# Second layer's first modulation product and first expert weights, moved to later tiles of the first output projection

## The chip, the cores and the metric

The kernel runs on one core of a Trainium2 chip. The core has five engines that work side by side: TensorE (PE in the profile, with its weight loads as PEld), VectorE (DVE), ScalarE (ACT), GpSimd (POOL) and SyncE (SP), which here issues nearly all DMAs. Each engine runs its own instructions in the order in which they stand in the program and waits on semaphores for the others. The metric is the time of one execution on the device in microseconds (us).

## The reference

Two layers work on 1024 latent tokens of 1024 channels, with 256 context tokens that the first layer reads. Cut to what matters here:

```
for i in (0, 1):
    sh1, sc1, g1, sh2, sc2, g2 = split(silu(c) @ ada_w[i] + ada_b[i], 6)    # ada_w[i]: 1024 x 6144
    h = modulate(rms_norm(x, norm_mix[i]), sh1, sc1)
    y = even_mixer(h, ...) if i == 0 else short_conv_mixer(h, ...)          # ends in an output projection
    x = x + g1 * y
    h2 = modulate(rms_norm(x, norm_ffn[i]), sh2, sc2)
    x = x + g2 * expert_choice_ffn(h2, router[i], w_gate[i], w_up[i], w_down[i])
return rms_norm(x, norm_final)

def expert_choice_ffn(h, router, w_gate, w_up, w_down):                     # 16 experts, 128 tokens each
    aff = softmax(h @ router)
    gate, idx = top_k(aff.T, 128)
    hid = silu(h[idx] @ w_gate) * (h[idx] @ w_up)
    y = (hid @ w_down) * gate
    return zeros_like(h).at[idx].add(y)
```

The split into six parts is made in three blocks of 2048 columns; block 0 of layer 1 holds `sh1` and `sc1`, which layer 1's first norm needs.

## The kernel before, in words

A product in float32 is made as three products of split operands (high by high, high by low, low by high), at lines 146 to 148. Weights come in granules of 1 MB: a load into a `raw` buffer (line 71, SyncE), a cast to `whi` on ScalarE (line 88), and the rest `wlo` on VectorE or GpSimd (line 89). The `raw` buffers come free when `wlo` has been made, the `whi` and `wlo` buffers when TensorE has used them.

The output projection of layer 0 runs in two passes over the eight tiles of 128 tokens. The second pass is the loop of `start0`: for each tile it loads the partial sum (`ox<-part`, line 664), multiplies (`po`), adds (line 673), transposes the sum (`pt<-ident,ox`, line 276), makes the router's logits (`lg`, lines 282 and 288) and their softmax (`sme`, lines 298 to 322), and writes the tokens' norm to a table (line 323) and the sum to `acc` (line 293). For the last two tiles (`late`) the norm's product is made on ScalarE (line 317) instead of VectorE. Then the tokens of each expert are chosen (lines 335 to 380).

The same loop takes along `ada`, the ten steps of `ada_blocks` for block 0 of layer 1: eight `products`, each of which loads 1 MB of `ada_w` (line 842) and multiplies it into `adsum` on VectorE (lines 845 and 847); `total`, which sums `adsum` over the partitions with four products on TensorE (`pad`, line 855); and `end`, which adds the bias row (line 866) and writes the block to `mods` (line 869). It is read back before layer 1 (`mod_rows<-mods`, line 1900). And it takes along `moe.fetch(early, 4)`, the loads of the first four granules of the first expert (line 71). All these loads take buffers of one pool of four, `raws`.

In `experts`, each expert has 48 products of gate and up (`gu`) on tokens that were gathered (`xg`), transposed on TensorE in two halves (`pt<-ident,xg`, line 411), and split to `xh` (line 140, ScalarE) and `xl` (line 141, VectorE); then the activation `sg`, its transposes (line 486), and 24 products with the down weights (`py`) one expert later. The 24 products of one half need that half's `xh`.

The order of the instructions is not the order of the code. A scheduler takes the instructions that are ready in its own model of time, by priority, where the place in the code is the priority; when a buffer comes free in that model, what waits for it may go ahead of what stands earlier. So a line that stands elsewhere in the code can leave the instructions where they were, and can move others that it has nothing to do with.

Of the kernel before, what the change touches and what calls it, by code (L numbers as in the profile page):

```python
# [648 lines left out]
def split_tile(co, pool, srcs):  # L649
    return split_into(co, *split_tiles(co, pool, sum(src.shape[1] for src in srcs)), srcs)  # L650


def out_project(co, t, mix, ws, x_src, pool, ps, done, half_done=lambda t, x, nh: None, tag="gu", x_pool=None):

    nc = co.nc
    st = {}

    def begin():
        st["mix"] = mix()
        st["x"] = x = (x_pool or pool).tile([P, D], F32, tag="ox", name=co.name("ox"), **({} if x_pool else {"bufs": 3}))
        nc.sync.dma_start(x, x_src[t * P : (t + 1) * P, :])

    def half(nh):
        x, m = st["x"], st["mix"]
        py = ps.tile([P, 512], F32, tag=tag, name=co.name("po"))
        for k, mk in enumerate(m):
            w = ws[nh][k // 4]  # L670
            co.mm3(py, mk, (w[0][:, k % 4, :], w[1][:, k % 4, :]), k == 0, k == len(m) - 1)
        sl = slice(nh * 512, (nh + 1) * 512)
        nc.vector.tensor_tensor(x[:, sl], x[:, sl], py, op=ALU.add)
        half_done(t, x, nh)

    return [begin, lambda: half(0), lambda: half(1), lambda: done(t, st["x"])]
# [896 lines left out]
def hybrid_dit_kernel(stack, tc, aps):  # L1573
# [29 lines left out]
    with ExitStack() as sa:  # L1603
# [71 lines left out]
        ada = [ada_steps(*b, sums, raws, ps, "ad", 4) for b in ((0, 1), (0, 2))] + [[]]  # L1675
# [152 lines left out]
    def start0(make, wpb, pool, ps, _):  # L1828
        moe = make()
        early = Weights(co, raws, wpa)  # L1830
        ada = ada_steps(1, 0, pool, raws, ps, "tr")
        x_pool = Cycle((Bufs(out_pool, 3), 3), (Bufs(pool, 2), 2))
        for i, (t, srcs) in enumerate(pass2.items()):
            for step in ada[2 * i : 2 * i + 2]:
                step()
            if i == 4:
                moe.fetch(early, 4)
            for step in out_project(
                co, t, lambda: split_tile(co, out_pool, srcs), ws, part, out_pool, ps,
                lambda t, x, late=i > 5: moe.route_tile(t, x, pool, ps, late), lambda t, x, nh: moe.route_half(t, x, nh, pool, ps), x_pool=x_pool,  # L1840
            ):
                step()
        mix0.close()
        kept_raws.insert(0, (stack.enter_context(pooled("more", 2, "right")), 2))
        return moe
# [69 lines left out]
    def mixed_raws():  # L1915
# [3 lines left out]
        return kept_cycle[0]  # L1919

    xs, moe0 = feed_forward(0, lambda wpb: None, start0, before_last)
    kept_splits.append(stack.enter_context(pooled("wps", 1, "right")))

# [70 lines left out]
```

## Time and profile before

| | us |
|---|---|
| median of 3 runs | 1860.47 |
| lowest and highest | 1858.13 and 1872.29 |
| the profiled execution's own time | 1875.52 |
| its span, first to last instruction | 1873.8 |

The page of the profile gives TensorE busy 1658.2 us (88% of the span), its weight loads 1338.6 us (71%), VectorE 1275.1 us (68%), ScalarE 903.3 us (48%), GpSimd 530.5 us (28%). The chain of work that ended last lies on TensorE for 47% of the span and on VectorE for 10%. Busy shares are means over stages that differ; a stage is read from its own window and from what ends the waits in it. The profiled execution took 15.05 us more than the median of the runs.

### The profile page before, as it was taken

To read this page: it belongs to the slowest core of one execution; us is meant where nothing else is said; L and a number is where in the kernel's file an instruction comes from. 1 tells how busy PE (TensorE), PEld (TensorE's weight loads), DVE (VectorE), ACT (ScalarE), POOL (GpSimd) and SP (SyncE) were. 2 spreads that over 40 slices of the span, in tenths; PEclk is the share of its full clock that TensorE was granted. 3 is DMA by queue.
4 is the path that set the end of the run, shared out by engine and by line. 5 is a ranking of instruction groups with operands and counts; after the bars stand their busy time and mean duration, and the time that the engine had idled before them with its cause. 6 is when DMAs were issued, how large, how long until landed. Compare 5 with 4: busy or idle time off the path is not lost.

```text
span 1873.8 us, 26253 instructions
## 1 busy us (share of the span) xinstructions
PE 1658.2 (88%) x9617; PEld 1338.6 (71%) x9617; DVE 1275.1 (68%) x1966; ACT 903.3 (48%) x1581; POOL 530.5 (28%) x549
## 2 busy tenths in 40 slices
PE   6999997878888893999989989999999769998995
PEld 2988875667886772778767767788887547776784
DVE  4628786656679766779778867354253558987897
ACT  3645332522753245878666552011132457876663
POOL 4310287462324027122111352000012432321123
PEclk7999999869998995899999999999999869998998
DMA  7517664648494957899999666531264369999995
GB/s 280 155 47 227 209 203 130 170 136 269 128 347 150 382 196 256 295 321 399 383 319 343 182 214 243 189 116 45 88 236 139 140 243 328 381 399 330 333 317 202
DMA packets 187671, 443.73 MB, mean 237 GB/s; under 512 B 46521, under 2 KB 108714, under 8 KB 158870
## 3 DMA queue, kind: packets, MB, share of 16 engines
q1 hardware_dynamic: 178470, 408.76, 61.0%
q0 software_dynamic: 9072, 33.30, 7.2%
q8 instruction: 76, 1.25, 0.3%
q14 instruction: 53, 0.43, 0.1%
HBM read 368.65 MB, written 73.35 MB: 236 GB/s over the span
## 4 chain that ended last, share of the span: by engine, by line
PE 47%; DVE 10%; issue 8%; DMA 7%; ACT 4%; POOL 1%; SPq 1%; DVEq 0%; ACTq 0%; POOLq 0%
PE pin L146 4%; PE pin L147 4%; PE pin L148 4%; PE gu L148 4%; PE gu L147 4%; PE gu L146 4%; PE po L146 3%; PE po L148 3%; PE po L147 3%; PE py L146 2%; PE py L147 2%; PE py L148 2%; DVE wlo L89 2%; ACT whi L88 2%; ACT oh L394 2%
## 5 line engine op out<-in xcount | busy, mean ns | idle before, releaser
L89 DVE TENSOR_TENSOR wlo<-raw,whi 128x2048 fp32r<-128x2048 f32 (+3 forms) x248 | 481.0, 1962 | 118.7 <-ACT whi L88 118.4
L88 ACT CAST whi<-raw 128x2048 fp32r<-128x2048 f32 (+3 forms) x268 | 423.7, 1613 | 210.4 <-PE pin L147 77.7
L146 PE MATMUL gu<-whi,xh 128*128 128x512 f32 x512 | 208.1, 409 | 17.7 <-ACT xh L140 16.9
L147 PE MATMUL gu<-wlo,xh 128*128 128x512 f32 x512 | 207.7, 406 | 3.1 <-DVE wlo L89 3.1
L148 PE MATMUL gu<-whi,xl 128*128 128x512 f32 x512 | 202.6, 409 | 0.2 <-DVE xl L141 0.2
L147 PE MATMUL pin<-h1T,whi 128*128 128x512 f32 x384 | 150.4, 393 | 0.0
L148 PE MATMUL pin<-h1T,wlo 128*128 128x512 f32 x384 | 150.2, 393 | 0.0
L146 PE MATMUL pin<-h1T,whi 128*128 128x512 f32 x384 | 148.9, 396 | 0.0
L522 POOL DMA_INDIRECT acc<-y,idx x31 | 80.0, 2579 | 209.9 <-DVE y L516 194.5
L400 POOL DMA_INDIRECT xg<-table,idx x32 | 57.8, 1806 | 286.3 <-ACT idx L398 272.6
L146 PEld LDWEIGHTS gu<-whi,xh 128*128 128x128 f32 x512 | 99.7, 195 | 39.5 <-ACT xh L140 19.2
L147 PEld LDWEIGHTS gu<-wlo,xh 128*128 128x128 f32 x512 | 99.4, 194 | 25.9 <-DVE wlo L89 5.0
L148 PEld LDWEIGHTS gu<-whi,xl 128*128 128x128 f32 x512 | 98.9, 193 | 20.5 <-DVE xl L141 0.6
L847 DVE SCALAR_TENSOR_TENSOR adsum<-raw,cs,adsum 128x512 f32<-128x512 f32 (+1 forms) x77 | 95.5, 1241 | 25.9 <-DMA raw<-in_ada_w_dram 25.5
L89 POOL TENSOR_TENSOR wlo<-raw,whi 128x1024 fp32r<-128x1024 f32 (+2 forms) x20 | 67.4, 3416 | 155.0 <-ACT whi L88 154.8
L146 PE MATMUL py<-whi,hh 128*128 128x512 f32 x256 | 102.5, 407 | 2.5 <-DVE y L516 1.3
L147 PE MATMUL py<-wlo,hh 128*128 128x512 f32 x256 | 102.0, 399 | 0.0
L148 PE MATMUL py<-whi,hl 128*128 128x512 f32 x256 | 101.7, 399 | 0.0
L146 PE MATMUL pq<-hT,whi 128*128 128x512 f32 (+1 forms) x256 | 97.0, 379 | 1.7 <-ACT last L1150 1.1
L148 PE MATMUL pq<-hT,wlo 128*128 128x512 f32 (+1 forms) x256 | 96.6, 377 | 0.0
L147 PE MATMUL pq<-hT,whi 128*128 128x512 f32 (+1 forms) x256 | 96.1, 376 | 0.0
L146 PE MATMUL po<-whi,mh 128*128 128x512 f32 x224 | 92.9, 416 | 3.0 <-ACT mh L140 2.3
(402 smaller groups left out, 3729.3 us busy)
## 6 DMA issues: line engine op xcount, KB each, us to landing
raw<-in_w_gate_dram SPq DMA_DIRECT2D x64, 1024.0 KB
raw<-in_w_up_dram SPq DMA_DIRECT2D x64, 1024.0 KB
raw<-in_w_down_dram SPq DMA_DIRECT2D x64, 1024.0 KB
raw<-in_ada_w_dram SPq DMA_DIRECT2D x32, 1024.0 KB
raw<-in_ada_w_dram SPq DMA_DIRECT2D x64, 256.0 KB
raw<-in_sc_w_in_dram SPq DMA_DIRECT2D x12, 1024.0 KB
table<-h SPq DMA_DIRECT2D x16, 520.0 KB
raw<-in_ev_w_in_dram SPq DMA_DIRECT2D x16, 512.0 KB
```

Source lines behind the costliest of these rows:

```text
L88: nc.scalar.copy(hi[:, part], raw[:, part])
L89: (lo_engine or e).tensor_sub(lo[:, part], raw[:, part], hi[:, part])
L146: nc.tensor.matmul(out, lhs[0], rhs[0], start=start, stop=False)
L147: nc.tensor.matmul(out, lhs[0], rhs[1], start=False, stop=False)
L148: nc.tensor.matmul(out, lhs[1], rhs[0], start=False, stop=stop)
L394: nc.scalar.activation(oh[:, t, :], co.places, AF.Sign, bias=before)
L400: nc.gpsimd.indirect_dma_start(out=xg, out_offset=None, in_=self.table[:, :], in_offset=bass.IndirectOffsetOnAxis(ap=idx, axis=0))
L522: self.scattered = self.nc.gpsimd.indirect_dma_start(out=self.acc[:, :], out_offset=bass.IndirectOffsetOnAxis(ap=idx, axis=0), in_=y, in_o ...
L847: nc.vector.scalar_tensor_tensor(st["sum"], raw, cs[:, k, 0:1], st["sum"], op0=ALU.mult, op1=ALU.add)
```

## The change

The ten steps of `ada` are taken two per tile: before in the first five turns of the loop (tiles 3, 4, 2, 5, 1), now in the last five (tiles 5, 1, 6, 0, 7). The call that fetches four granules moves from the fifth turn to the seventh.

```diff
         for i, (t, srcs) in enumerate(pass2.items()):
-            for step in ada[2 * i : 2 * i + 2]:
+
+            for step in ada[2 * (i - 3) : 2 * (i - 2)] if i >= 3 else []:
                 step()
-            if i == 4:
+            if i == 6:
                 moe.fetch(early, 4)
             for step in out_project(
```

Three places show what became of it in the order of the instructions.

First, SyncE in the second pass, where the last loads of `ada_w` and the first granules stand. Before:

```order
L842 DMA raw_7185<-in_ada_w_dram 128x2048
L842 DMA raw_7188<-in_ada_w_dram 128x2048
L71 DMA raw_7285<-in_w_gate_dram 128x2048
L664 DMA ox_7013<-part 128x1024
L1780 DMA part<-ox_6790 128x1024
L71 DMA raw_7287<-in_w_up_dram 128x2048
L293 DMA acc_79<-ox_6920 128x1024
L71 DMA raw_7289<-in_w_gate_dram 128x2048
L71 DMA raw_7291<-in_w_up_dram 128x2048
```

Now:

```order
L842 DMA raw_7446<-in_ada_w_dram 128x2048
L842 DMA raw_7449<-in_ada_w_dram 128x2048
L71 DMA raw_7452<-in_w_gate_dram 128x2048
L664 DMA ox_6997<-part 128x1024
L1780 DMA part<-ox_6790 128x1024
L71 DMA raw_7454<-in_w_up_dram 128x2048
L293 DMA acc_79<-ox_6910 128x1024
L71 DMA raw_7456<-in_w_gate_dram 128x2048
L71 DMA raw_7458<-in_w_up_dram 128x2048
```

The names have other numbers, and the rows are the same: each load stands where it stood, and so it is with all eight loads of `ada_w`. On SyncE the one row of the pass that moved is `mods<-adrows`, from ahead of the third of the eight `table` rows to behind the fourth. On VectorE the eight products stand where they stood, and the row of line 866 stands 25 rows later; on TensorE the four `pad` products stand some 55 rows later, still inside the pass, and the transposes and logits of the last tiles are laid out a little differently.

Second, TensorE in layer 0's experts, at the first tokens of expert 10 (`pt_9412` and `xh_9417` are its first half, `sg_9466` is the activation of expert 9, `py` is expert 8's down product). Before:

```order
L411 MATMUL pt_9412<-ident,xg_9031 128x128 x4
L146 MATMUL gu_9544<-whi_9548,xh_9417 128x512
L147 MATMUL gu_9544<-wlo_9549,xh_9417 128x512
L146 MATMUL gu_9545<-whi_9566,xh_9417 128x512
L147 MATMUL gu_9545<-wlo_9567,xh_9417 128x512
L411 MATMUL pt_9457<-ident,xg_9031 128x128 x4
L146 MATMUL py_9482<-whi_9472,hh_9346 128x512
L147 MATMUL py_9482<-wlo_9473,hh_9346 128x512
L148 MATMUL py_9482<-whi_9472,hl_9347 128x512
```

Now:

```order
L411 MATMUL pt_9412<-ident,xg_9031 128x128 x4
L146 MATMUL gu_9544<-whi_9548,xh_9417 128x512
L147 MATMUL gu_9544<-wlo_9549,xh_9417 128x512
L146 MATMUL gu_9545<-whi_9566,xh_9417 128x512
L147 MATMUL gu_9545<-wlo_9567,xh_9417 128x512
L411 MATMUL pt_9457<-ident,xg_9031 128x128 x4
L486 MATMUL pt_9511<-ident,sg_9466 128x128 x4
L148 MATMUL gu_9544<-whi_9548,xl_9418 128x512
L146 MATMUL gu_9544<-whi_9548,xh_9417 128x512
L147 MATMUL gu_9544<-wlo_9549,xh_9417 128x512
```

Up to the second row of transposes nothing moved since the pass. Then the activation of expert 9 is transposed ahead of expert 8's down products, and 17 products of expert 10 follow it. From here the two programs differ. Between the transposes of an expert's first half and the first product that uses them stood, for experts 9 to 13, 0, 0, 1, 20 and 11 products; now 0, 0, 24, 21 and 21.

Third, TensorE in layer 1's experts, where expert 8's first half is transposed (`pt_14774`, which becomes `xh_14779`; `xh_14654` is expert 7). Before:

```order
L148 MATMUL gu_14736<-whi_14785,xl_14655 128x512
L146 MATMUL gu_14736<-whi_14785,xh_14654 128x512
L411 MATMUL pt_14774<-ident,xg_14393 128x128 x4
L147 MATMUL gu_14736<-wlo_14786,xh_14654 128x512
L148 MATMUL gu_14736<-whi_14785,xl_14655 128x512
L146 MATMUL gu_14737<-whi_14803,xh_14654 128x512
L147 MATMUL gu_14737<-wlo_14804,xh_14654 128x512
```

Now:

```order
L411 MATMUL pt_14774<-ident,xg_14393 128x128 x4
L148 MATMUL gu_14737<-whi_14803,xl_14655 128x512
L146 MATMUL gu_14737<-whi_14803,xh_14654 128x512
L147 MATMUL gu_14737<-wlo_14804,xh_14654 128x512
L148 MATMUL gu_14737<-whi_14803,xl_14655 128x512
L411 MATMUL pt_14819<-ident,xg_14393 128x128 x4
L146 MATMUL gu_14906<-whi_14910,xh_14779 128x512
L147 MATMUL gu_14906<-wlo_14911,xh_14779 128x512
L146 MATMUL gu_14907<-whi_14928,xh_14779 128x512
L147 MATMUL gu_14907<-wlo_14929,xh_14779 128x512
```

Before, 14 products stood between those transposes and the first one that uses `xh_14779`; now 4 do. For experts 8 to 13 of layer 1 the numbers were 14, 0, 0, 1, 20 and 11; now they are 4, 4, 15, 0, 21 and 0.

## Rows read from the trace of the kernel before

**Rows 1.** Stages: us, busy (x) of PE, PEld, DVE, ACT, POOL; PEclk, DMA, GB/s.

```profile
636.00:712.00 76.00, 68.49 (x434) 50.10 (x433) 53.94 (x113) 31.16 (x86) 21.73 (x15) 0.97 0.64 248
...
753.00:1062.00 309.00, 293.46 (x1386) 238.58 (x1387) 258.20 (x183) 226.22 (x269) 63.12 (x29) 0.96 0.92 335
...
1524.00:1843.00 319.00, 303.26 (x1441) 246.34 (x1442) 265.43 (x190) 229.09 (x280) 67.70 (x30) 0.97 0.91 326
```

**Rows 2.** Waits of SyncE in layer 0's experts: us in total, times, longest.

```profile
SPq L71 <- DVE wlo L89: 218.1, 69, 11.2
```

**Rows 3.** Waits of ScalarE in the same stretch.

```profile
ACT whi L88 <- PE py L148: 28.6, 14, 6.8
...
ACT whi L88 <- PE gu L148: 10.9, 7, 2.9
```

**Rows 4.** TensorE in layer 0's experts: [idle before <-releaser].

```profile
965.21 0.50 PE L146 MATMUL gu<-whi,xh 128*128 128x512 f32 x1 [0.44 <-ACT xh L140]
...
967.08 0.74 PE L411 MATMUL pt<-ident,xg 128*128 128x128 f32 x4 [0.67 <-ACT idx L398]
968.52 0.71 PE L486 MATMUL pt<-ident,sg 128*128 128x128 f32 x4 [0.69 <-DVE xl L141]
...
1005.31 0.50 PE L146 MATMUL gu<-whi,xh 128*128 128x512 f32 x1 [1.28 <-ACT xh L140]
...
1007.91 0.55 PE L147 MATMUL gu<-wlo,xh 128*128 128x512 f32 x1 [1.63 <-DVE wlo L89]
```

**Rows 5.** TensorE in layer 1's experts, the same.

```profile
1687.83 0.79 PE L146 MATMUL gu<-whi,xh 128*128 128x512 f32 x1 [2.64 <-ACT xh L140]
...
1690.20 0.80 PE L147 MATMUL gu<-wlo,xh 128*128 128x512 f32 x1 [0.72 <-DVE wlo L89]
...
1710.41 0.75 PE L411 MATMUL pt<-ident,xg 128*128 128x128 f32 x4 [0.87 <-DVE hl L141]
1714.06 0.51 PE L146 MATMUL gu<-whi,xh 128*128 128x512 f32 x1 [2.91 <-ACT xh L140]
...
1716.97 0.80 PE L146 MATMUL py<-whi,hh 128*128 128x512 f32 x1 [0.55 <-DVE y L516]
...
1776.84 0.49 PE L146 MATMUL gu<-whi,xh 128*128 128x512 f32 x1 [0.82 <-ACT whi L88]
```

**Rows 6.** SyncE's queue in order of time: start us, us, DMA issue.

```profile
578.44 0.33 SPq L842 DMA_DIRECT2D raw<-in_ada_w_dram  x1
...
636.78 3.33 SPq L842 DMA_DIRECT2D raw<-in_ada_w_dram  x2
642.06 0.33 SPq L71 DMA_DIRECT2D raw<-in_w_gate_dram  x1
...
686.41 0.55 SPq L869 DMA_DIRECT2D mods<-adrows  x1
...
697.09 0.32 SPq L323 DMA_DIRECT2D table<-h  x1
...
734.79 0.38 SPq L1900 DMA_DIRECT2D mod_rows<-mods  x1
```

**Rows 7.** VectorE in order of time, the last ada product and its sum.

```profile
653.13 2.35 DVE L847 SCALAR_TENSOR_TENSOR adsum<-raw,cs,adsum 128x2048 f32<-128x2048 f32 x1
...
685.70 0.68 DVE L866 TENSOR_TENSOR adrows<-adrows,pad 128x512 f32<-128x512 f32 x1
```

**Rows 8.** TensorE in order of time, the pass of layer 0.

```profile
684.49 1.04 PE L855 MATMUL pad<-adsum,ones 128*32 128x512 f32 x8
```

**Rows 9.** ScalarE in order of time, the last tiles of that pass.

```profile
709.82 1.13 ACT L317 ACTIVATE h<-ox,rstd 128x1024 f32<-128x1024 f32 x1
710.86 0.39 ACT L307 ACTIVATE sme<-sme,sm 128x128 f32<-128x128 f32 x1
```

**Rows 10.** Two windows in layer 1's experts, columns as in rows 1.

```profile
1710.00:1720.00 10.00, 6.14 (x19) 4.57 (x20) 7.95 (x8) 4.75 (x6) 4.26 (x2) 0.74 0.96 351
1720.00:1730.00 10.00, 10.00 (x50) 8.20 (x50) 4.51 (x3) 6.45 (x12) 0.00 (x0) 0.92 0.74 207
```

## The prediction

> **What bounds the kernel now.** I read the stages first. In the second pass TensorE is busy 68.49 of 76.00 us, and VectorE 53.94 [rows 1]: the pass is TensorE's, and work that is put elsewhere inside it finds no hole to fill. The eight loads and products that the edit names are the smaller matter there; the experts that follow are the larger, since they take 309 us in layer 0 and 319 us in layer 1 with TensorE busy 293.46 and 303.26 [rows 1]. What is left to win or lose in them is 15.5 and 15.7 us of idleness, and the half clock that comes with it.
>
> Then I asked who waits for whom there. SyncE's loads of weights wait for `wlo`, 69 times and 218.1 us [rows 2], so the transfers are held back by buffers that are full. ScalarE's casts wait for TensorE's products, 28.6 and 10.9 us [rows 3], and no row has them wait for a load. So TensorE sets the pace, and the splits and the loads follow it. Last I read what TensorE itself waits for: the `xh` of tokens that it transposed just before [rows 4, 5].
>
> **The loads and the products of the modulation: 0.** The code asks for them three tiles later, but the order shows all eight loads and the four early granules in the rows where they stood, and the eight VectorE products too. The first load is issued at 578.44, before the second pass begins, and the last pair from 636.78 on, with the first granule at 642.06 [rows 6]. What lets them go is a free buffer, and that is the same as before. The last product starts at 653.13 and takes 2.35 us [rows 7], and stays. I put nothing on it. Bounds: nothing excludes that a load meets a wait of another kind, but no row on SyncE ahead of it differs, so both ends are 0.
>
> **The sum over partitions and its write: 0, between -1.0 and +1.0.** The four `pad` products take 1.04 us [rows 8], and stand some 55 rows later now. A step of 1.04 us that moves within a stretch in which TensorE is the bound changes nothing; at most it falls into an idle gap (-1.04) or delays the last tile by itself (+1.04). The row of line 866, at 685.70 [rows 7], moves 25 rows down; it takes 0.68 us of a VectorE that is busy 71% here (53.94 of 76.00 us [rows 1]). The write to `mods` was issued at 686.41; it now follows the fourth `table` row, which was issued at 697.09, and the block is read back at 734.79 [rows 6]. So it is still some 37 us early. Queued behind it on SyncE are `table` and `acc` rows of the last tiles, whose data come later than the sum of line 866.
>
> **The last tiles: 0, between -1.0 and +1.1.** Before, the two late tiles end together: the second tile's exponent waits at 709.82 until the first tile's norm product of 1.13 us is through, and starts at 710.86 [rows 9]. Now one late tile is done whole on ScalarE ahead of the other's softmax. If it comes 1.04 us earlier, the wait goes (-1.04); if not, the other's softmax waits for the product's 1.13 us. The rows speak for neither, so I take 0.
>
> **Layer 0's experts: -3.1, between -4.7 and +2.9.** Up to expert 10's first transposes TensorE's rows are the same. From there on the transposes of experts 11, 12 and 13 have 24, 21 and 21 products behind them before their tokens are wanted, where 1, 20 and 11 stood. A window of 10 us at nearly full clock holds 50 products, some of them small [rows 10], so one takes 0.2 us at least and 21 take 4.2 us, more than the longest such wait, 2.91 [rows 5]. The waits in this stretch are 0.44, 0.67 and 0.69 around 965 us, which hang on expert 11's transposes, 1.28 at 1005.31 on expert 13's, and 1.63 at 1007.91 on a `wlo` [rows 4]. The first four go: 0.44 + 0.67 + 0.69 + 1.28 = 3.08. The fifth is a split and need not; with it 4.71. On the other side, expert 9's activation is now transposed right behind another transpose and 17 products of expert 10 come ahead of the down products that covered them; if their `xl` or a split is late, that is one wait of the usual size, 2.9.
>
> **Layer 1's experts: +1.6, between -6.7 and +14.5.** Here the same spots cost, before, for expert 9: 2.64 + 0.72 = 3.36; for expert 10: 0.87 + 2.91 + 0.55 = 4.33; for expert 11 the three waits of layer 0 repeat, 0.44 + 0.67 + 0.69 = 1.80 [rows 4]; for expert 13: 0.82 [rows 5]. In all 10.3 us. Now experts 11 and 13 have nothing between the transposes and their first use, and experts 8 and 9 have four products; experts 10 and 12 have 15 and 21 and should be free. A spot with nothing between cost 3.36 to 4.33 where ScalarE had casts of weights ahead of the `xh`, as it has in the new order, so 3.85 each; four products of 0.2 us take 0.8 off a wait of 2.9, which leaves 2.1 each. 2 x 3.85 + 2 x 2.1 = 11.9, and 11.9 - 10.3 = +1.6. Low end: all four spots as cheap as half of expert 11's, 0.9 each: 3.6 - 10.3 = -6.7. High end: each spot at the full price of expert 10's, where the window from 1710 holds 19 products against 50 in the next one, at a granted clock of 0.74 (the engine ran at 1.2 GHz for part of it, right after it had stood idle) [rows 10]: (50 - 19) / 50 x 10 = 6.2 us, and 4 x 6.2 - 10.3 = +14.5.
>
> **The sum.** 0 + 0 + 0 - 3.1 + 1.6 = -1.5 us. Against the profiled execution's own 1875.52 that is 1874.0. That execution lies 15.05 above the median and above the slowest of the three runs, so I carry the difference and not the time: 1860.47 - 1.5 = 1859.0. A measurement of this kernel can tell about 1%, or 18.6 us, from no change (its own three runs lie 14.2 apart), and the sum is a tenth of that.
>
> **The rivals.** *Layer 1 pays (slower).* The mechanism is the half clock behind a short wait: each of the four spots in experts 8 to 13 costs 6.2 us as expert 10 did. For it: the window from 1710 [rows 10]. Against it: only one spot of four went so before, and expert 11's cost 1.80. It decides from the third spot at full price on: two at 6.2 and two at 2.1 are 16.6, or +6.3. At the full +14.5 with -3.1 in layer 0 it gives 1872. The Trainium skill, "TensorE: Matmul & The Clock Gate", section "HAM oscillation — how this bites in real kernels", says that a wait that recurs throttles the array each time, so that every turn starts at the slow clock. By that rule every one of the four spots is dear, and 1872 would be the forecast; the trace agrees at expert 10 and does not at expert 11, which cost 1.80.
>
> *The short waits all go (faster).* Layer 0 gains 4.7, the pass 1.0, and layer 1's spots are cheap, 6.7: 1860.5 - 12.4 = 1848. For it: TensorE is the bound, so each wait counts whole. Against it: ScalarE's order in layer 1 puts up to five casts ahead of expert 11's `xh`.
>
> *The transfers set the pace of the experts, and nothing moves.* Then a wait that goes on TensorE comes back as a wait for weights: 1860.5. For it: the DMA share is 0.92 and 0.91 [rows 1]. Against it: 335 and 326 GB/s, and loads that wait for buffers [rows 1, 2]. The Trainium skill, "Perfetto Trace Analysis", section "Roofline", puts the ceiling of one core at its 16 DMA engines, about 435 GB/s in all. By that figure the stage has a quarter of the rate left, and this rival falls; the trace agrees so far as no cast waits for a load.
>
> *The change does what it says on the chip after all*, and the loads come three tiles later: excluded by the order, which the queues follow.
>
> **How the numbers follow.** My forecast, 1859, with its neighbours from 1852 to 1866: 0.55. Layer 1 pays, 1866 to 1877: 0.17. The waits all go, 1846 to 1852: 0.12. Transfers set the pace, 1860.5: 0.10. What I have not seen, on either side, the loads that move among it: 0.06. The lows add up to -1.0 - 1.0 - 4.7 - 6.7 = -13.4, or 1847; the highs, +1.0 + 1.1 + 2.9 + 14.5 = +19.5, or 1880, which needs all of them at once. The range is 1846 to 1876. Faster by over 1% would be under 1842, more than all the lows: 0.07. Slower by over 1% is above 1879, only at the end of the highs: 0.07. Within 1%: 0.86.
>
> **What would show it.** In the profile after: the `ada_w` loads from about 578 to 640 and the last `adsum` at about 653, as before; the `pad` product near 700; the choice of tokens starting within 1.5 us of 712; in layer 0's experts no waits for `xh` behind expert 10; in layer 1's, waits at experts 8, 9, 11 and 13 and none at 10. I am wrong if the loads move, if the pass ends more than 2 us elsewhere, or if the two stages of experts change by more than 5 and 15 us; then the coupling of ScalarE's casts with TensorE's releases does more than these rows show.

## The result: slower by 0.57%, 10.6 us

Of 20 runs each, the changed kernel takes 1876.6 us in the median (1869.24 to 1881.56) and the kernel before 1863.7 (1858.13 to 1872.29). The ratio is 1.0057, with a 95% interval from 1.0045 to 1.0068: 10.6 us, from 8.4 to 12.7 (the two medians by themselves lie 12.9 us apart). I had forecast 1859, a gain of 1.5 us, with a range up to 1876. I had started from 1860.47, the median of three runs of before; with 20 it is 1863.7, so 3.2 us of the distance to 1876.6 lie in the start and not in the change. I had also put the least that can be told at about 1%; the interval reaches some 0.1% to each side. The profiled execution of after took 1879.88 us, its span is 1878.0.

The stages of after, in windows as in [rows 1], each moved to where the stage now begins:

```profile
632.00:708.00 76.00, 69.08 (x434) 50.73 (x433) 54.00 (x113) 31.46 (x88) 22.89 (x15) 0.97 0.67 251
748.00:1057.00 309.00, 292.07 (x1397) 235.64 (x1398) 259.14 (x187) 225.89 (x269) 68.69 (x29) 0.97 0.92 335
1518.00:1837.00 319.00, 297.63 (x1403) 239.73 (x1404) 259.54 (x184) 228.99 (x279) 63.33 (x29) 0.96 0.90 324
```

In these windows the pass and layer 0's experts look much as they did; the second window ends before the last products of layer 0, of which more below. In layer 1's experts TensorE gets through 1403 instructions in 319 us, where it got through 1441 [rows 1]. The loss is there.

SyncE's queue of after, in order of time:

```profile
574.56 0.33 SPq L842 DMA_DIRECT2D raw<-in_ada_w_dram  x1
...
632.66 3.33 SPq L842 DMA_DIRECT2D raw<-in_ada_w_dram  x2
637.93 0.33 SPq L71 DMA_DIRECT2D raw<-in_w_gate_dram  x1
...
698.52 0.55 SPq L869 DMA_DIRECT2D mods<-adrows  x1
```

VectorE of after, the last product of the modulation and the row of line 866:

```profile
649.09 2.35 DVE L847 SCALAR_TENSOR_TENSOR adsum<-raw,cs,adsum 128x2048 f32<-128x2048 f32 x1
...
697.80 0.69 DVE L866 TENSOR_TENSOR adrows<-adrows,pad 128x512 f32<-128x512 f32 x1 [0.44 <-PE pad L855]
```

The loads, the granules and the products stand as before, 4 us earlier on this execution's clock [rows 6, 7]; only the sum and the write to `mods` are later, by 12 us on the clock and so by 16 against the rest. The choice of tokens, its first row (line 335) and the row `dg` (line 352) on VectorE, before:

```profile
712.14 1.28 DVE L335 TENSOR_SCALAR_CACHE_REDUCE junk<-v,cand 128x1024 bf16<-128x1024 f32 x1
...
732.08 2.30 DVE L352 TENSOR_SCALAR dg<-ident,cand 128x16 f32<-128x16 f32 x1
```

And in after:

```profile
708.14 1.28 DVE L335 TENSOR_SCALAR_CACHE_REDUCE junk<-v,cand 128x1024 bf16<-128x1024 f32 x1
...
728.07 0.85 DVE L352 TENSOR_SCALAR dg<-ident,cand 128x16 f32<-128x16 f32 x1
```

From the first load to the first row of the choice of tokens it is 133.58 us (708.14 - 574.56) and was 133.70 (712.14 - 578.44). So what the change names costs nothing. From that row to layer 0's first product, though, the six executions with after's order there (after, force11to13, undo_l1, undo_swap, undo_early, copies_late_after) take 39.5 to 39.7 us, and the eleven with before's 41.1 to 42.5: some 2.2 us are won. The row `dg` is where it shows: it takes 0.74 to 0.90 us in the six and 2.30 to 3.66 in the eleven, and ends 0.03 us behind a split of weights on GpSimd (`wlo`, line 89) in all seventeen. In the six that split begins 3.6 to 3.8 us ahead of `dg`, in the eleven 0.9 to 2.2.

To compare experts across executions I count the products with gate, up and down weights (lines 146 to 148, 1152 in each layer) in the timeline. Layer 1, in us, with the experiments that follow; the two columns of us are from one profiled execution of each kernel:

| kernel | ratio to before, 95% interval | 1st to 577th product | 577th to last |
|---|---|---|---|
| before | 1 | 154.6 | 164.5 |
| after | 1.0057 (1.0045 to 1.0068) | 159.7 | 170.0 |
| fetch5 | 0.9999 (0.9981 to 1.0017) | 155.4 | 164.0 |
| fetch6 | 0.9995 (0.9976 to 1.0013) | 152.2 | 163.9 |
| force11to13 | 1.0084 (1.0059 to 1.0110) | 158.7 | 171.6 |
| force_late | 1.0065 (1.0042 to 1.0087) | 158.6 | 168.6 |
| undo_l1 | 0.9999 (0.9982 to 1.0016) | 153.1 | 164.1 |
| do_l1 | 1.0058 (1.0040 to 1.0076) | 159.1 | 171.7 |
| do_early | 1.0036 (1.0017 to 1.0055) | 158.4 | 164.1 |
| do_late | 1.0028 (1.0014 to 1.0041) | 151.2 | 170.0 |
| do_swap | 1.0025 (1.0007 to 1.0042) | 155.1 | 164.2 |
| undo_swap | 1.0052 (1.0034 to 1.0070) | 153.8 | 170.1 |
| do_rest | 1.0018 (0.9998 to 1.0039) | 158.5 | 162.7 |
| undo_early | 1.0030 (1.0010 to 1.0050) | 151.6 | 169.1 |
| copies_late | 0.9947 (0.9928 to 0.9966) | 149.9 | 165.2 |
| copies_late_after | 1.0005 (0.9985 to 1.0026) | 148.7 | 168.7 |
| copies_turn | 1.0047 (1.0032 to 1.0063) | 148.6 | 171.8 |

TensorE in layer 1's experts in after, the waits at the first products of expert 1 (experts count from 0) and at experts 9, 10, 11 and 13:

```profile
1534.97 0.51 PE L146 MATMUL gu<-whi,xh 128*128 128x512 f32 x1 [1.48 <-ACT xh L140]
...
1537.41 0.80 PE L148 MATMUL gu<-whi,xl 128*128 128x512 f32 x1 [1.24 <-DVE xl L141]
...
1686.98 0.67 PE L147 MATMUL gu<-wlo,xh 128*128 128x512 f32 x1 [2.30 <-DVE wlo L89]
...
1708.19 0.50 PE L146 MATMUL gu<-whi,xh 128*128 128x512 f32 x1 [1.45 <-ACT xh L140]
...
1731.70 0.79 PE L146 MATMUL gu<-whi,xh 128*128 128x512 f32 x1 [2.84 <-ACT xh L140]
...
1735.31 1.13 PE L411 MATMUL pt<-ident,xg 128*128 128x128 f32 x4 [1.53 <-DVE xl L141]
...
1776.62 0.51 PE L146 MATMUL gu<-whi,xh 128*128 128x512 f32 x1 [2.00 <-ACT xh L140]
...
1779.06 1.04 PE L411 MATMUL pt<-ident,xg 128*128 128x128 f32 x4 [1.24 <-DVE xl L141]
```

Counted off, the row at 1686.98 is the 604th product, in expert 9; the one at 1708.19 is the 673rd, the first of expert 10; those at 1731.70 and 1776.62 are the 745th and the 889th, the first of experts 11 and 13. So of the spots that I had named, 9, 11 and 13 wait. Expert 8, for which I had put 2.1 us, waits for nothing, and expert 10, which I had put down as free, waits 1.45 us for `xh`. The 15 products of the order do stand between its transposes and their use. But on ScalarE the cast to `xh`, at 1707.58, comes behind three casts of weights and these rows:

```profile
1705.23 2.45 ACT L394 ACTIVATE oh<-places,aff 128x128 f16<-128x128 f16 x8
```

The first two rows of the list I had not foreseen: before's profile shows none for `xh` or `xl` at that place. ScalarE there, before:

```profile
1531.41 1.91 ACT L88 CAST whi<-raw 128x2048 fp32r<-128x2048 f32 x1 [0.99 <-issue]
1533.71 1.92 ACT L88 CAST whi<-raw 128x2048 fp32r<-128x2048 f32 x1 [0.39 <-PE gu L148]
1538.34 0.19 ACT L403 COPY aff<-xg 128x1 f32<-128x1 f32 x1 [2.71 <-DMA xg<-table,idx]
1538.44 0.58 ACT L140 CAST xh<-pt 128x512 fp32r<-128x512 f32 x1
```

And in after:

```profile
1524.73 1.92 ACT L88 CAST whi<-raw 128x2048 fp32r<-128x2048 f32 x1 [0.61 <-issue]
1532.44 0.19 ACT L403 COPY aff<-xg 128x1 f32<-128x1 f32 x1 [5.79 <-DMA xg<-table,idx]
1532.54 1.90 ACT L88 CAST whi<-raw 128x2048 fp32r<-128x2048 f32 x1
1534.34 0.58 ACT L140 CAST xh<-pt 128x512 fp32r<-128x512 f32 x1
```

Two neighbours have changed places. The copy of a gathered gate (line 403) waits for its gather; before, the second cast of weights was done in that time. Now the cast stands behind the copy: ScalarE stands still for 5.79 us, and `xh` comes 1.90 us after the copy instead of right after it.

The same has happened once more, some 80 us after the first product: the copy of expert 6's gate has gone ahead of a cast of weights that stood ahead of it. The copy before, and then in after:

```profile
1604.76 0.19 ACT L403 COPY aff<-xg 128x1 f32<-128x1 f32 x1 [5.06 <-DMA xg<-table,idx]
```

```profile
1601.64 0.19 ACT L403 COPY aff<-xg 128x1 f32<-128x1 f32 x1 [6.77 <-DMA xg<-table,idx]
```

### The profile page after: what moved, and what is told of

The parts are those of the page before. It is cut to its first block, busy times and chain, and to the rows that moved or that the text cites. A ratio compares the mean times of both kernels' runs of the same rounds, so it can differ in the third digit from the quotient of the medians.

```text
span 1878.0 us, 26243 instructions
## 1 busy us (share of the span) xinstructions
PE 1656.6 (88%) x9617; PEld 1334.0 (71%) x9617; DVE 1277.8 (68%) x1966; ACT 903.3 (48%) x1581; POOL 534.1 (28%) x549
## 5 line engine op out<-in xcount | busy, mean ns | idle before, releaser
L89 POOL TENSOR_TENSOR wlo<-raw,whi 128x1024 fp32r<-128x1024 f32 (+2 forms) x20 | 66.8, 3387 | 151.7 <-ACT whi L88 151.6
```

The costliest lines, as they stand in the source:

```text
L89: (lo_engine or e).tensor_sub(lo[:, part], raw[:, part], hi[:, part])
```

## The experiments

### The granules' half, and transposes put earlier

The first theory (A) was the prediction's own rival: the late spots of layer 1 cost more than I had put on them. **fetch5** and **fetch6** are the kernel before with the fetch alone moved:

```diff
-            if i == 4:
+            if i == 6:
                 moe.fetch(early, 4)
```

(`i == 5` in fetch5.)

> The kernel before with the fetch of four granules one tile later (at i == 5), the products left alone. The order of the instructions is the same as before's on all five engines. Both theories: ratio 1.000, between 0.9985 and 1.0015. It shows what the measurement tells from nothing, and its trace is a second sample of before's order: if the first eight experts of layer 1 take 153.6 us to their 576th product as before, the 159.7 us of after are the change's; if they take up to 160, they are scatter of single executions.

> Only the second half of the change: the fetch at i == 6, the eight products where they were. The order keeps the pad products and the mods write ahead as before, and gives layer 1's experts the order of after, instruction for instruction; layer 0's from expert 10 on nearly so. Theory A (the order of the late experts costs it): as after, ratio 1.004 to 1.007. Theory B (it is the moved modulation in the pass, or the first experts of layer 1 as they follow from it): ratio 1.000 to 1.002, since pad and mods stand as before.

Both came out as before, 0.9999 and 0.9995. The expectation of fetch6 is wrong on the order: with the fetch alone moved, the rows of all five engines are before's, as with fetch5. So its time says nothing between A and B. It shows that the moved fetch by itself does nothing, and gives a third sample of before's order. The three take 152.2 to 155.4 us to the 577th product of layer 1, and after 159.7. Single executions of one order do scatter there: undo_swap and do_rest below have the same rows up to expert 7 and take 153.8 and 158.5.

**force11to13** is after, and **force_late** before, with transposes held ahead of the products of the expert before (in force_late the condition is experts 8 to 15 of both layers; the lines that hand over the two instructions are left out):

```diff
-                        co.mm3(pa, (hi[:, k, :], lo[:, k, :]), (g[0][:, k, :], g[1][:, k, :]), half == k == 0, half == 1 and k == 3)
+                        mm = co.mm3(pa, (hi[:, k, :], lo[:, k, :]), (g[0][:, k, :], g[1][:, k, :]), half == k == 0, half == 1 and k == 3)
+                        if self.li and e in (10, 11, 12) and half and rows and k == 0:
+                            co.order(self.turn, mm)
```

> The kernel after, with one constraint on TensorE's order in layer 1 only: the transposes of the first half of experts 11, 12 and 13 stand ahead of the second-half products of the expert before, so that 24 products lie between them and their first use instead of 0, 21 and 0. Theory A: the two spots of 4.2 and 3.6 us by the trace go, 5 to 8 us of the 10.6, ratio 1.001 to 1.003. Theory B: the spots are as cheap as the prediction's sum had them beside before's own, and the ratio stays at 1.005 to 1.006.

> The kernel before, with that constraint for experts 8 to 15 of both layers: 24 products at least between the first half's transposes and their use, where before has 14, 0, 0, 1, 20 and 11. Theory A: the waits for xh of both layers go with the half clock behind them, 4.7 us in layer 0 and 10.3 in layer 1 by the waits alone: ratio 0.990 to 0.994, faster than both kernels. Rival (transfers and splits set the pace, and TensorE's waits only come back in another place): 0.998 to 1.002.

Theory A foresaw gains, and neither has one: force11to13 is at 1.0084 where after is at 1.0057, and force_late at 1.0065 where before is at 1. In force_late the waits for `xh` in the late experts went, and others came. TensorE in force_late, in layer 1 from expert 7 on:

```profile
1676.04 1.13 PE L412 MATMUL pt<-ident,xg 128*128 128x128 f32 x4 [4.27 <-DVE hl L141]
...
1750.70 0.51 PE L147 MATMUL gu<-wlo,xh 128*128 128x512 f32 x1 [1.97 <-DVE wlo L89]
...
1853.19 0.79 PE L563 MATMUL plast<-xl,xh 128*128 128x512 f32 x1 [4.65 <-DVE raw L565]
```

The early transposes wait 4.27 us for `hl`: they write a buffer of the pool `tr`, which has two, and `hl` still reads one. Then the splits are late (`wlo`), and the sums after the last expert. But each constraint also made the scheduler lay out other rows anew, so neither run says what a spot costs. That called for kernels in which nothing else moves.

### Layer 1 in a given order

The next eight kernels hold every engine in an order that is written down, from layer 1's choice of tokens on: before's, after's, or a mixture. The edges bind the issue order only.

```diff
+def pin_orders(tc, nc):
...
+    for rows in json.loads(zlib.decompress(base64.b85decode(PINNED))).values():
+        for earlier, later in zip(rows, rows[1:]):
+            tc.add_manual_dep(traced[base + later], traced[base + earlier].name, no_wait, reason="order")
...
         hybrid_dit_kernel(tc, args)
+        pin_orders(tc, nc)
```

> The kernel after, with the instructions of layer 1 (from its choice of tokens on) held on every engine in the order of the kernel before; the pass, layer 0 and the mixer stay as in after. Theory C (all of the loss is layer 1's order, its first experts included): ratio 0.999, between 0.997 and 1.001. Rival P (the pass with the moved pad and mods, or layer 0, causes it): as after, 1.0045 to 1.0068.

> The converse: the kernel before, with layer 1 held in the order of after; everything ahead of it as before. Theory C: ratio 1.006, between 1.004 and 1.008. Rival P: 0.9985 to 1.0015.

**undo_l1** gives 0.9999 and **do_l1** 1.0058. Theory C holds and rival P falls: the whole loss is the order of layer 1, and what stands in front of it comes out even.

**do_early** and **do_late** divide it between experts 4 and 7, where both orders agree.

> The kernel before, and of after's order in layer 1 only what lies in the first three experts: two swaps of neighbours on VectorE, three on ScalarE, three moves on TensorE. The first of them puts the copy of a gathered row's gate, which waits for the gather, ahead of a cast of weights on ScalarE. By the traces after is 5 us behind at the 480th product (135.1 against 130.0, 130.8 and 127.7 us). Theory C1 (a copy that waits for a transfer, with casts behind it, costs several us): ratio 1.0025, between 1.0015 and 1.004, with waits for xh and xl of some 2.7 us near 17 us after the first product. Theory C2 (only the late experts count): 0.999 to 1.001, and the 5 us are scatter.

> The kernel before, and of after's order in layer 1 only what lies from expert 7 on. By the traces the stretch from the 576th to the last product takes 170.0 us in after and 164.5, 164.1 and 163.9 in three executions of before's order. Theory C1: ratio 1.003, between 1.0015 and 1.0045, so that the two parts add up to do_l1. Theory C2: 1.0045 to 1.007, all of it. My recorded sum put it at +1.6 us, which would be 1.001.

1.0036 and 1.0028: both parts count, together 1.0064 beside do_l1's 1.0058. TensorE of do_early, at the place of after's first two waits:

```profile
1528.04 0.50 PE L146 MATMUL gu<-whi,xh 128*128 128x512 f32 x1 [1.16 <-ACT xh L140]
...
1530.48 0.80 PE L148 MATMUL gu<-whi,xl 128*128 128x512 f32 x1 [1.24 <-DVE xl L141]
```

C1 named these two waits with 2.7 us near 17 us after the first product; they are 2.40 us, at 16.3 and 18.8. In the traces the parts do not overlap. To the 577th product the six executions with before's first experts take 151.2 to 155.4 us (mean 153.0), the four with all of after's 158.4 to 159.7 (159.0; force11to13 is one). From the 577th on, seven with before's late experts take 162.7 to 164.5 (163.9), five with after's 169.1 to 171.7 (170.2).

### One pair of neighbours

**do_swap** is before with the pair on ScalarE exchanged, **undo_swap** is after with it put back, **do_rest** is do_early without it, and **undo_early** is after with all early moves put back. The edit of do_swap, in the rows of ScalarE's order:

```diff
 L88 CAST whi_13765<-raw_13763 128x2048
-L88 CAST whi_13783<-raw_13781 128x2048
 L403 COPY aff_13619<-xg_13621 128x1
+L88 CAST whi_13783<-raw_13781 128x2048
 L140 CAST xh_13655<-pt_13650 128x512
```

> The kernel before, with one pair of neighbours exchanged and nothing else: on ScalarE, in layer 1's first expert, the copy of a gathered gate (line 403, it waits for a gather) now stands ahead of one cast of weights (line 88), as in after. TensorE keeps before's order, so that the two products that after has put ten places later meet the late cast at once. Theory C1 (a waiting copy with a cast behind it): ratio 1.003, between 1.0015 and 1.005, most of do_early's 1.0036. Theory C3 (the copy gives up only time that ScalarE has, and the other small moves make the loss): 0.9985 to 1.001.

> The kernel after, with that one pair put back and all else of layer 1 held as in after. Theory C1: the 5.6 us that the first experts lose go for the most part, ratio 1.0028, between 1.001 and 1.0045. Theory C3: as after, 1.005 to 1.007.

> do_early without the exchanged pair: the kernel before with the other small moves of after's first three experts in layer 1. Theory C1 (the pair carries the early loss): 0.9995 to 1.0015. Theory C4 (the other moves carry half of it or more): 1.002 to 1.004.

> The kernel after with all moves of layer 1's first three experts put back, the late experts in after's order. Both theories: 1.0028 as do_late, between 1.0015 and 1.004, if the parts add up; beside undo_swap's 1.0052 it shows what the other moves cost in after. If it comes out near 1.005 too, the early part costs after nothing and the parts do not add up.

do_swap costs 0.0025, as C1 had it. do_rest costs 0.0018 with an interval down to zero, between the two theories. undo_early is at 1.0030, where both had it. undo_swap is at 1.0052, against C1, though in its trace the two waits are gone and the 577th product comes at 153.8 us. That execution is the fastest of its six, and the ratio stays unexplained. By the ratios alone it is open how the early loss divides.

The traces divide it. From the 1st to the 73rd product of layer 1, the five executions with the pair exchanged (after, do_l1, do_early, do_swap, force11to13) take 24.7 to 26.7 us (mean 25.5), and the nine without it, the copies in their old places, 20.5 to 21.9 (21.2). The pair costs 4.3 us, or 0.0023. And do_rest, which was to show the other moves without a copy, is not without one: it keeps the second copy ahead of its cast, where ScalarE waits 7.51 us in its trace. From the 289th to the 361st product the six executions with that second pair exchanged (after, do_l1, do_early, undo_swap, do_rest, force11to13) take 20.1 to 22.2 us (20.8), and the eight without 18.3 to 20.1 (19.0): 1.8 us. The two make 6.1 us, as much as the 6.0 that the first experts lose. Between the two stretches these groups of six and eight scatter by 3 us and differ by 0.2 in the mean; behind them, force_late apart, they agree within 0.1. So do_rest does not tell C1 from C4.

### The copies out of the way

In **copies_late** and **copies_late_after** the order of before, or of after, is held from layer 0's choice of tokens on, and each gate copy is put behind the second `xh` cast of its own expert:

```diff
+    rows = pinned["Activation"]
+    for copy, casts in tc.gates:
+        if at[copy.name] in rows:
+            rows.remove(at[copy.name])
+            rows.insert(rows.index(at[casts[1].name]) + 1, at[copy.name])
```

> The kernel before, its order held, with all 32 gate copies of both layers moved down on ScalarE, each behind the second xh cast of its own expert, which needs the same gather. Theory C1: the 35 us in which ScalarE stands before gathers go, and with them the waits of TensorE that hang on casts in the first experts of each layer, some 2 to 4 us in each: ratio 0.9965, between 0.994 and 0.999, faster than both kernels. Rival: ScalarE has that time anyway, and only the one copy of after met a cast that TensorE needs: 0.999 to 1.001.

> The kernel after, its order held, with all 32 gate copies moved behind the second xh cast of their own expert, as in copies_late. Theory C1: the early part goes with them, and what is left over copies_late is the late part, 0.9947 + 0.0028 = 0.9975, between 0.996 and 0.999. Theory C4: the early moves stay dear, 0.9947 + 0.0057 = 1.0004, between 0.999 and 1.002.

copies_late takes 0.9947 of before's time, 1855.91 us in the median: faster than both kernels. ScalarE waits for no gather there any more. By the trace layer 0's 1152 products take 314.6 us, where eight executions of before's order took 316.2 to 321.6, and layer 1's 315.1, where four took 316.1 to 319.5. Its window at the place where after lost 2.72 us:

```profile
1528.00:1538.00 10.00, 10.00 (x49) 8.32 (x48) 8.78 (x6) 8.70 (x9) 0.00 (x0) 1.00 0.88 329
```

The same place in after:

```profile
1530.00:1540.00 10.00, 7.28 (x28) 5.54 (x27) 4.25 (x3) 7.53 (x7) 0.00 (x0) 0.85 0.54 177
```

49 instructions in 10 us against 28. copies_late_after shows 148.7 us to the 577th product, beside 149.9: with the copies out of the way the early moves of after cost nothing in the trace, which is C1. Its ratio, 1.0005, is C4's number. The 0.0058 between the two ratios is 0.0030 more than the late part. Part of it lies ahead of layer 1: layer 0's products take 318.5 us against 314.6, and the choice of tokens to the first product 39.5 against 41.4, which leaves 2 us or 0.0010. The intervals are 0.002 to each side, so the rest is not settled.

**copies_turn** adds, in both layers, the first-half transposes of experts 9 to 11, 16 products ahead of their use, with their `xh` and `xl` up to two rows earlier, in a held order.

> The same, and in both layers the first-half transposes of experts 9, 10 and 11 are put 16 products ahead of their first use instead of 0, 0 and 1, their xh and xl by up to two rows ahead of casts and splits of weights. If the spots are as dear as the prediction read them (3.36, 4.33 and 1.80 us in layer 1, 1.80 in layer 0): another 0.004 below copies_late. Rival (what force_late showed: the wait for xh comes back as a wait for wlo, since ScalarE and VectorE are the ones that are late there): within 0.0015 of copies_late, or above it.

1.0047, so 0.0100 above copies_late. The rival holds, and more than it said. TensorE in its layer 1:

```profile
1677.67 1.13 PE L415 MATMUL pt<-ident,xg 128*128 128x128 f32 x4 [2.33 <-DVE hl L143]
...
1687.25 0.50 PE L149 MATMUL gu<-wlo,xh 128*128 128x512 f32 x1 [2.97 <-DVE wlo L89]
...
1707.10 1.13 PE L415 MATMUL pt<-ident,xg 128*128 128x128 f32 x4 [4.53 <-DVE hl L143]
```

The transposes wait for `hl`, as in force_late, now with nothing moved but them and their `xh` and `xl`. Put 16 products earlier, they find their buffer still taken.

## Why the prediction was wrong

**Loads, products, pad, mods, last tiles: right.** Each was put at 0. The stretch from the first load to the choice of tokens kept its length to 0.12 us, and undo_l1, which has all of it, gives 0.9999. That number is a balance, though: the 2.2 us won in the choice of tokens, for which I had no term, and a loss of about as much in layer 0's experts.

**Layer 0's experts, -3.1: the waits went, and others came.** The five waits that I listed [rows 4] are gone. But the one at expert 10's own first product, which I took as equal in both, grew from 2.90 us before to 4.71:

```profile
942.47 0.50 PE L146 MATMUL gu<-whi,xh 128*128 128x512 f32 x1 [2.90 <-ACT xh L140]
```

```profile
936.81 0.79 PE L146 MATMUL gu<-whi,xh 128*128 128x512 f32 x1 [4.71 <-ACT xh L140]
```

It is 4.70 or 4.71 us in all six executions of after's order. TensorE in after, behind it to the last expert:

```profile
958.35 0.50 PE L147 MATMUL gu<-wlo,xh 128*128 128x512 f32 x1 [0.81 <-DVE wlo L89]
...
978.06 0.75 PE L411 MATMUL pt<-ident,xg 128*128 128x128 f32 x4 [0.51 <-DVE xl L141]
...
1014.98 0.49 PE L146 MATMUL gu<-whi,xh 128*128 128x512 f32 x1 [0.31 <-ACT whi L88]
1016.42 0.50 PE L148 MATMUL gu<-whi,xl 128*128 128x512 f32 x1 [0.94 <-DVE xl L141]
...
1041.26 0.50 PE L148 MATMUL gu<-whi,xl 128*128 128x512 f32 x1 [0.43 <-DVE xl L141]
...
1044.45 0.50 PE L147 MATMUL gu<-wlo,xh 128*128 128x512 f32 x1 [0.61 <-DVE wlo L89]
...
1056.24 0.79 PE L147 MATMUL py<-wlo,hh 128*128 128x512 f32 x1 [1.84 <-DVE wlo L89]
```

These add up to 5.45 us, more than the 4.71 that left. Layer 0's 577th to 1057th product takes 141.1 us in five executions of after's order and 143.3 in eight of before's, a gain of 2.2. The last 96 products take 28.4 to 28.5 us against 23.3, a loss of 5.1. Together that is +2.9 where I had -3.1: the sign is wrong, and only the choice of tokens, which won 2.2, hides it from undo_l1. I had counted the waits that go, and did not follow the order into expert 10's own tokens and the last two experts, where the splits are late.

**Layer 1's experts, +1.6: the step that failed.** Measured by do_l1 it is +0.0058, or 10.8 us. Two things are wrong in it.

The larger: a term is missing. I put nothing on the first eight experts, since I let TensorE set the pace, with the casts to follow it. ScalarE's order had two copies of gates there that had gone ahead of a cast, and TensorE and VectorE had a few small moves. That is +6.0 us by the traces, +0.0036 by do_early. A warning was in before's trace: [rows 3] show the waits of the casts alone, and in layer 1's experts (1524 to 1843 us) the same view has one for a transfer:

```profile
ACT aff L403 <- DMA xg<-table,idx: 17.9, 4, 8.3
```

No cast waits for a load of weights, as I wrote, but casts stand behind a copy that waits for a gather. The rival "Layer 1 pays" was nearest in time with 1872, but its mechanism covers only the other half.

The smaller: the late experts are mis-sized, by waits outside the spots that I counted. The spots themselves fell partly elsewhere: at 9, 11 and 13 as I said, at 10, which I had free, and not at 8, for which I had 2.1 us. To count products between transposes and use was not enough at expert 10, where ScalarE came late. By the prediction's own measure, the windows of after at experts 9, 10, 11 and 13:

```profile
1685.00:1695.00 10.00, 8.00 (x32) 6.37 (x32) 8.87 (x7) 3.03 (x5) 3.15 (x2) 0.83 1.01 421
1706.00:1716.00 10.00, 7.96 (x35) 5.65 (x34) 9.17 (x7) 8.70 (x14) 1.04 (x1) 1.00 0.96 366
1728.00:1738.00 10.00, 5.63 (x19) 4.09 (x18) 10.00 (x8) 6.21 (x7) 0.60 (x1) 0.68 0.98 365
1774.00:1784.00 10.00, 6.76 (x26) 5.19 (x25) 9.07 (x8) 4.86 (x5) 2.20 (x2) 0.83 1.01 417
```

And of before at experts 9, 11 and 13 (expert 10's is in [rows 10]):

```profile
1684.00:1694.00 10.00, 6.63 (x22) 4.71 (x21) 8.95 (x7) 8.13 (x9) 0.98 (x1) 0.67 1.01 405
...
1734.00:1744.00 10.00, 8.21 (x39) 6.32 (x38) 10.00 (x10) 6.64 (x9) 1.67 (x2) 1.00 0.89 342
1776.00:1786.00 10.00, 8.68 (x41) 7.07 (x41) 10.00 (x8) 7.12 (x9) 3.46 (x2) 1.00 0.96 374
```

Against 50 in a full window, after's spots cost 3.6 + 3.0 + 6.2 + 4.8 = 17.6 us, where I had 11.9, and before's 5.6 + 6.2 + 2.2 + 1.8 = 15.8, where I had 10.3. The half clock was left out on both sides, so the difference, +1.8, is about my +1.6. That agreement is luck, since 8 and 10 were both wrong and made up for each other. And the late part is +6.2 us by the traces, and +0.0028 or 5.2 us by do_late. Followed product by product, the five executions with after's late experts fall back by 2.4 us between the 817th and the 841st, in expert 12, where after's TensorE has waits of 0.56 and 0.64 us for `xl` and `wlo`, and by 2.1 us in the last 120. I had counted nothing at these places.

The Trainium skill, "TensorE: Matmul & The Clock Gate", section "HAM oscillation — how this bites in real kernels", has a wait that recurs throttle the array each time, in a kernel with longer waits than these: the windows of after agree at experts 9, 11 and 13 (0.83, 0.68, 0.83) and not at 10 (1.00).

**What would show it.** The loads, the last `adsum` (649.09) and no waits for `xh` behind layer 0's expert 10 were as written. Layer 1's spots were not: 9, 10, 11 and 13 wait, and 8 does not. The choice of tokens came at 708.14 and not within 1.5 us of 712, since this execution runs 4 us ahead from before the pass on. Layer 1 changed by 10.6 us in the two profiles, under the 15 that I had set as a sign of being wrong. The clause that did hold is the last: the coupling of ScalarE's casts with TensorE does more than the rows that I had chosen show.

## What to carry to other kernels

When an edit reshuffles a scheduler's order, compare all engines over the whole program, also where TensorE's rows are equal, and look first for an instruction that waits for a transfer and has changed places with work that others need, and for every such pair: one cost 0.25% here, and putting all such copies behind a use that needs the same transfer gained 0.53%. To find which of many moves costs, hold the order of every engine and exchange one piece at a time; a single constraint on a free scheduler moves other things (force11to13, force_late). And before putting an instruction earlier, ask whether its buffer is free by then: these transposes' was not.

## What the runs showed of the hardware that was not expected

In layer 1 the gather that the first exchanged copy needs ends ScalarE's wait 12.9 to 15.1 us after the first product, in fourteen executions with either place of the cast: the landing does not move with the order. A cast ahead of the copy runs in time that is lost anyway, and one behind it comes that much later.

The full clock is lost behind a wait, and not by each. In after, the wait of 2.30 us at expert 9 was followed by a window at 0.83, those of 2.84 and 1.53 at expert 11 by one at 0.68, while the window around the 1.45 us at expert 10 stayed at 1.00.

Where no transfer is waited for, executions of one order repeat closely: the last 96 products of layer 0 agree within 0.1 us in eight. The first 577 products of layer 1, where ScalarE waits for gathers, spread over 4.2 us in six.

The row `dg` of the choice of tokens (128x16 on VectorE) took between 0.74 and 3.66 us, and ended 0.03 us behind a split of weights on GpSimd in each of seventeen executions. When that split began, and not the row itself, decided how long it took; the 2.2 us that after wins ahead of layer 0 lie there.
